# A mixture-of-experts stretch: splits one load later in the program, rows brought back later, evacuations one piece behind

## The chip, the cores and the metric

The kernel runs on one core of a Trainium2 chip. A core has a matrix engine (TensorE, PE in the profile), a vector engine (VectorE, DVE), a scalar engine (ScalarE, ACT), GpSimd (POOL) and a sync engine (SyncE, SP) that starts transfers here. The engines run side by side, each in the order of its own program, and wait for each other by semaphores. The metric is the device time of one execution in microseconds (us).

## The reference

Two decoder layers over 256 positions of width 1024, in float32. Layer 0 mixes with windowed attention beside a short convolution and then applies a dense SwiGLU. Layer 1 mixes with a gated linear recurrence and then applies a mixture of eight experts, two for each position. All that the change touches lies in the last part:

```python
top_logits, top_idx = lax.top_k(xf @ w_router, 2)
gates = softmax(top_logits)
# for each expert e, over the positions that chose it:
hb = silu(xb @ w_gate[e]) * (xb @ w_up[e])     # (rows,1024)@(1024,3584), twice
yb = hb @ w_down[e]                            # (rows,3584)@(3584,1024)
out = x + sum over the two chosen experts of gate * yb
```

The weights of the eight experts are 8 x 3 x 1024 x 3584 numbers of 4 bytes, 352 MB, and each is read once.

## The kernel before, in words

Each float32 operand is written as a high part H, rounded to the matrix engine's fp32r type by an ACT copy, and a low part L, the rest, by a DVE subtraction. A product is then a few fp32r matmuls (H with H, H with L, L with H).

The experts are sorted by how many positions chose them. Three get room for 128 rows and are called heavy (turns 0, 3 and 6 of the program), five get 64 rows and are called light (turns 1, 2, 4, 5 and 7). In a light expert H and L of the rows stand beside each other in the 128 columns, so that a weight chunk needs four matmuls for each piece, in a heavy one six. The hidden width 3584 is cut in seven parts f of 512. The program's list `order` holds the 56 (expert, f) items: three heavy items first, then cycles of light, heavy, light.

The weights of an item are six loads of 1 MB (two each for gate, up and down), and each load feeds two pieces. The list `pieces` holds, for each item, four gate pieces, four up pieces, and then the four down pieces of the item before, so a cycle of three items is 36 pieces or 18 loads. The main loop (L1203 and after) issues for each piece n, in this order: its matmuls (`products`), the evacuations of a finished gate or up bank (`follow`), whatever was put off to this piece (`later`, filled by `at`), and the splits of the next loads, as many as `AHEAD` allows (`prepare`). This part of the kernel is under a manual schedule: each engine gets its instructions in just that order. So the place of a split relative to the small operations is a matter of the code, and an ACT or DVE operation that waits for TensorE holds up every split behind it.

- `prepare` and `hl_of` (L256, L257): the split of one load, an ACT copy of 128x2048 into H and a DVE subtraction into L. H and L come from four pairs of buffers (`N_HL`), and a pair is free when the matmuls of its load are done.
- The loads land in seven 1 MB buffers in turn (five of the ring `w` and two of `b`). SP issues a transfer (L205, L961) when the DVE subtraction of the load that had the buffer before is done.
- `follow`: for a heavy item Silu out of the gate bank (L1147) and a DVE product with the up bank (L1156), then `turn` five pieces after the last up piece, which transposes the hidden part into the shape of a left operand. For a light item copies out of both banks (L1149, L1160), then `turn_light` five pieces after (matmuls L1103, Silu L1105, product L1106) and `split_light` nine pieces after (L256 and L257 on `b`). The down pieces, 13 to 16 pieces after, read the result.
- When the last down pieces of an expert are done, `out_parts` scales and splits its output (ACT L1121, DVE L1122), and `combine` brings its rows back to their positions (matmuls L1129 and L1130 into a `pz` bank) and adds them into x (DVE L1132). Four such quarters follow an expert, one and two pieces after each half of `out_parts`.
- `gather` (matmuls L1025 and L1035, copies L1027 and L1038), `factors` and `back` prepare the next expert's rows, selection factors and transposed selection.
- There are two `pz` banks for all of these, four `pa` banks for the outputs of the experts under way, and two `pw` banks for gate and up.

Of the kernel before, what the change touches and what calls it, by code (L numbers as in the profile page):

```python
# [14 lines left out]
AF = mybir.ActivationFunctionType  # L15
# [5 lines left out]
S = 256  # L21
# [10 lines left out]
N_HL = 4  # L32
# [17 lines left out]
FAR = 1024  # L50


AHEAD = N_HL
FIRST = 1
SECOND = 2
TURN = 5

TURNS8 = N_RING + 2
TURNS4 = TURNS8 + 2
# [54 lines left out]
def body(ctx, tc, x_d, w_d, prm_d, bv_d, rt_d, out_d):  # L114
# [33 lines left out]
    def pz():  # L148
        return psp.tile([P, 512], F32, tag="z", name=nm("pz"))
# [761 lines left out]
    def experts(rest):  # L911
# [30 lines left out]

        parts = {}
        loads = len(pieces) // 2
        later = {}
        regs = {}
        sel, xg, fac, pts, psum, hid, ys, yp = {}, {}, {}, {}, {}, {}, {}, {}
# [67 lines left out]
        def gather(u, b):  # L1015

            ps = units[u]
            o = (pa if ps[0] == 0 and not rest else pz)()
            if ps[0] in heavy:

                a, b = b // 2, b % 2
                for j in range(4):
                    d = (4 * b + j) * P
                    for t in R2:
                        T.matmul(o[:, j * P:(j + 1) * P], (xh3, xl3)[a][:, t, d:d + P], sel_of(ps[0], t),  # L1025
                                 start=t == 0, stop=t == 1)
                A.activation(xg[ps[0]][a][:, b * 512:(b + 1) * 512], o, AF.Copy)  # L1027
                return

            o = o[:, 0:256 * len(ps)].rearrange("p (e j a s) -> p e j a s", e=len(ps), j=2, a=2)  # L1030
            for j in R2:
                d = (2 * b + j) * P
                for a in R2:
                    for t in R2:
                        T.matmul(o[:, :, j, a, :], (xh3, xl3)[a][:, t, d:d + P], sel[u][:, t, :, 0:64],  # L1035
                                 start=t == 0, stop=t == 1)
            for e, p in enumerate(ps):
                A.activation(xg[p][:, b * 256:(b + 1) * 256], o[:, e, :, :, :].rearrange("p j a s -> p (j a s)"), AF.Copy)  # L1038

        def factors(p, cols):  # L1040

            o = pz()
            sc = scl if rest or p == 0 else sclp
            for t in R2:
                T.matmul(o[:, cols], sel_of(p, t).bitcast(F32), sc[:, t, p, cols], start=t == 0, stop=t == 1)
            if p not in fac:
                fac[p] = sm.tile([P, 2], F32, tag="gs", name=nm("gs"), bufs=6)
            V.tensor_copy(fac[p][:, cols], o[:, cols])

        def back(p):  # L1050

            o = pz()
            for t in R2:
                T.transpose(o[:, t * P:(t + 1) * P], sel_of(p, t).bitcast(F32), ident)
            pt = b1(F32R)
            A.activation(pt, o[:, 0:S], AF.Copy)
            pts[p] = pt
# [9 lines left out]
        def products(n):  # L1067
            m, p, f, i = pieces[n]
            h, l = parts.pop(n)
            if m in "gu":  # L1070
                if i == 0:
                    psum[m] = pw()
                for j in range(2):
                    c = slice(j * 512, (j + 1) * 512)
                    k = 2 * i + j
                    r = slice(k * P, (k + 1) * P)
                    a = (xg[p][0][:, r], xg[p][1][:, r]) if p in heavy else xg[p][:, r]
                    mm(psum[m], a, h[:, c], l[:, c], k == 0, k == KC - 1)
            else:
                if f == 0 and i == 0:  # L1080
                    ys[p] = pa(), pa()
                for j in R2:
                    k = 2 * (i % 2) + j
                    r = slice(k * P, (k + 1) * P)
                    o = slice(j * 512, (j + 1) * 512)
                    a = (hid[p, f][0][:, r], hid[p, f][1][:, r]) if p in heavy else hid[p, f][:, r]
                    mm(ys[p][i // 2], a, h[:, o], l[:, o], f == 0 and k == 0, f == NF - 1 and k == 3)

        def turn(p, f, sg):
            o = pz()  # L1090
            for k in range(4):
                T.transpose(o[:, k * P:(k + 1) * P], sg[:, k * P:(k + 1) * P], ident)
            hh, hlo = b2(F32R), b2(F32R)
            hl_of(o, hh, hlo)
            hid[p, f] = hh, hlo

        def turn_light(p, f, g, u):

            o = pz()
            for j, src in enumerate((g, u)):  # L1100
                for k in range(4):
                    c = j * S + k * 64
                    T.matmul(o[:, c:c + 64], src[:, k * P:(k + 1) * P], ii, start=True, stop=True)  # L1103
            s = b2()
            A.activation(s[:, 0:S], o[:, 0:S], AF.Silu)  # L1105
            V.tensor_mul(s[:, S:], o[:, S:], s[:, 0:S])  # L1106
            hid[p, f] = s

        def split_light(p, f):
            h = b2(F32R)  # L1110
# [4 lines left out]
        def out_parts(p, c):  # L1115

            gs = fac[p][:, 0:1]
            if c == 0:
                yp[p] = b4(F32R), b4(F32R)
            yh, yl = (y[:, c * 512:(c + 1) * 512] for y in yp[p])  # L1120
            A.activation(yh, ys[p][c], AF.Copy, scale=gs)  # L1121
            V.scalar_tensor_tensor(yl, ys[p][c], gs, yh.bitcast(F32), OP.mult, OP.subtract)  # L1122

        def combine(p, i):
            yh, yl = yp[p]
            o = pz()
            for j in range(2):
                d = slice((2 * i + j) * P, (2 * i + j + 1) * P)
                T.matmul(o[:, j * S:(j + 1) * S], yh[:, d], pts[p], start=True, stop=False)  # L1129
                T.matmul(o[:, j * S:(j + 1) * S], yl[:, d], pts[p], start=False, stop=True)  # L1130
            v = x_sb[:, 2 * i:2 * i + 2, :]
            V.tensor_add(v, k3(o, 2), v)  # L1132
            if p == order[-1][0]:
                q = (nc.sync, nc.scalar)[i % 2]
                q.dma_start(out_d[:, i * 512:(i + 1) * 512].rearrange("p (k s) -> p k s", k=2), v)

        def at(n, fn, *a):
            later.setdefault(min(n, len(pieces) - 1), []).append((fn, a))

        def follow(n):  # L1140

            m, p, f, i = pieces[n]
            if m == "g" and i == 3:
                sg = b2()
                if p in heavy:

                    A.activation(sg, psum["g"], AF.Silu, scale=fac[p][:, 1:2])  # L1147
                else:
                    A.activation(sg, psum["g"], AF.Copy, scale=fac[p][:, 1:2])  # L1149
                psum["sg"] = sg  # L1150
            elif m == "u" and i == 3:
                sg = psum["sg"]

                last = (p, f) == order[-1]
                if p in heavy:
                    V.tensor_mul(sg, psum["u"], sg)  # L1156
                    at(n + (1 if last else TURN), turn, p, f, sg)
                else:
                    u = b2()
                    A.activation(u, psum["u"], AF.Copy)  # L1160
                    at(n + (1 if last else TURN), turn_light, p, f, sg, u)
                    at(n + (3 if last else TURN + 4), split_light, p, f)
            elif m == "d" and i % 2 and f == NF - 1:
                out_parts(p, i // 2)
                for j in R2:
                    at(n + 1 + j, combine, p, i - 1 + j)

        if not rest:
            at(1, places)
# [15 lines left out]
        with tc.manual_schedule():  # L1185
            for n in range(FIRST):
                prepare(n)
            if not rest:
                router(3)
                low = by_token(3)  # L1190
                choices()

                A.activation(rw[:, 4, 0, 0:1], ones[:, 0:1], AF.Silu)
            choose(0)
            if not rest:
                squares(3)
            for n in range(FIRST, SECOND):
                prepare(n)
            for b in (0, 2):
                gather(0, b)  # L1200
            if not rest:
                low()
            ready = SECOND  # L1203
            for n in range(len(pieces)):
                products(n)
                if n == 1:
                    for b in (1, 3):
                        gather(0, b)
                if n == 0 and not rest:
                    norm()  # L1210
                if n == 3:
                    factors(0, slice(1, 2))
                follow(n)
                for fn, a in later.pop(n, ()):
                    fn(*a)
                while ready < min((n + 1) // 2 + AHEAD, SECOND + n + 1, loads):
                    prepare(ready)
                    ready += 1
# [97 lines left out]
```

## Time and profile before

| what | value |
|---|---|
| median of 3 runs | 1376.69 us (1376.37 to 1381.61) |
| the profiled execution's own time | 1379.48 us |
| its span in the profile | 1377.7 us |
| TensorE busy, share of the span | 95% |
| VectorE busy | 83% |
| ScalarE busy | 71% |
| read from memory | 424.77 MB, 309 GB/s over the span |

The profiled execution took 2.8 us more than the median of the runs, and 1.8 us of its time lie outside the span. A busy TensorE is not a full one, since the ends of matmuls are modelled: one of 512 columns is shown with some 390 ns, though the next one starts 0.23 us after it.

How the views below are read. The windows view gives for each stretch its length, then for PE, PE's weight loads, DVE, ACT and POOL the busy time with the number of instructions, then the granted TensorE clock as a share, the busy share of the DMA engines, and the GB/s that they moved. The transfers by line give the number of issues, the size of one and the median us from issue to landing. The chain of waits gives the start, the length and the line of each step of the chain that ended last. The timeline gives start, length, engine, line and tiles of instructions in order, and in brackets the idle time before it with what ended it. The waits give who waited for whom, the us in total, how often, and the longest.

### The profile page before, as it was taken

The page shows a single profiled execution, that of the slowest core. Times are in us where ns is not written, and L with a number is a line of the kernel's source. Part 1 is how long each engine was busy: PE and PEld are TensorE (multiplying, and loading weights), DVE is VectorE, ACT ScalarE, POOL GpSimd, SP SyncE. Part 2 cuts the span into 40 slices and gives each one's busy share as a digit, 9 for nine tenths or more (in the row PEclk, how much of TensorE's full clock was granted, in tenths as well). Part 3 has the DMA queues.
Part 4 walks back from the last instruction along what each step waited for, and adds up shares of the span by engine and source line. Part 5 has one row for each costly group of instructions (what it writes and reads, how often), then busy time and mean ns, then how long its engine had stood idle before and what let it go on. Part 6 is the DMA issues. An engine that isn't in the chain of part 4 may idle for free.

```text
span 1377.7 us, 19891 instructions
## 1 busy us (share of the span) xinstructions
PE 1303.7 (95%) x7727; PEld 1140.7 (83%) x7727; DVE 1137.9 (83%) x1051; ACT 976.4 (71%) x939; POOL 4.2 (0%) x29
## 2 busy tenths in 40 slices
PE   8999999999998999999899999999989999999997
PEld 7799999999998778778678777777768878787775
DVE  6677655555786789999989998999988999989996
ACT  6445444444587678898778888788867887878893
POOL 1000000000000000000000000000000000000000
PEclk9999999999999999999999999999999999999999
DMA  7444555555434579999989999999998999989992
GB/s 293 145 147 168 186 182 183 183 181 183 173 122 183 215 279 375 419 421 421 420 299 382 422 420 393 351 414 420 419 397 306 382 421 421 405 327 422 421 418 80
DMA packets 61446, 427.19 MB, mean 310 GB/s; under 512 B 7200, under 2 KB 7200, under 8 KB 11296
## 3 DMA queue, kind: packets, MB, share of 16 engines
q1 hardware_dynamic: 60624, 425.22, 78.1%
q8 instruction: 62, 1.02, 0.3%
q10 hardware_dynamic: 720, 0.62, 0.1%
q14 instruction: 40, 0.33, 0.1%
HBM read 424.77 MB, written 1.05 MB: 309 GB/s over the span
## 4 chain that ended last, share of the span: by engine, by line
PE 67%; DVE 15%; issue 9%; ACT 8%; DMA 0%; DVEq 0%; SPq 0%; ACTq 0%
DVE L L257 11%; PE pw L236 9%; PE pw L237 9%; PE pw L238 9%; ACT H L256 4%; PE pz L1103 4%; PE pw L1064 3%; PE pa L237 3%; PE pw L1065 3%; PE pa L238 3%; PE pa L236 3%; PE pa L319 3%; PE pa L317 3%; PE pa L318 3%; PE pa L1064 3%
## 5 line engine op out<-in xcount | busy, mean ns | idle before, releaser
L257 DVE TENSOR_TENSOR L<-w,H 128x2048 fp32r<-128x2048 f32 (+1 forms) x243 | 537.8, 2241 | 53.9 <-ACT H L256 53.4
L256 ACT ACTIVATE H<-w 128x2048 fp32r<-128x2048 f32 (+1 forms) x243 | 452.3, 1877 | 52.8 <-PE pw L238 25.5
L231 ACT ACTIVATE H<-w 128x1024 fp32r<-128x1024 f32 (+1 forms) x138 | 140.2, 1039 | 153.7 <-issue 139.9
L257 DVE TENSOR_TENSOR L<-b,H 128x2048 fp32r<-128x2048 f32 (+1 forms) x102 | 222.1, 2200 | 12.0 <-ACT H L256 11.8
L1064 PE MATMUL pw<-H,b 128*128 128x512 f32 x560 | 222.2, 397 | 0.0
L1065 PE MATMUL pw<-L,b 128*128 128x512 f32 x560 | 218.5, 390 | 0.0
L232 DVE TENSOR_TENSOR L<-w,H 128x1024 fp32r<-128x1024 f32 (+1 forms) x138 | 164.1, 1205 | 56.1 <-ACT H L231 56.1
L256 ACT ACTIVATE H<-b 128x2048 fp32r<-128x2048 f32 (+1 forms) x102 | 187.0, 1844 | 16.6 <-PE pw L238 8.8
L236 PE MATMUL pw<-b,H 128*128 128x256 f32 x672 | 191.6, 286 | 2.1 <-DVE b L622 1.1
L237 PE MATMUL pw<-b,H 128*128 128x256 f32 x672 | 191.3, 285 | 0.0
L238 PE MATMUL pw<-b,L 128*128 128x256 f32 x672 | 191.2, 285 | 0.0
L1064 PE MATMUL pa<-H,b 128*128 128x512 f32 x280 | 113.7, 406 | 26.3 <-DVE b L257 26.3
L236 PE MATMUL pw<-H,b 128*128 128x512 f32 x336 | 133.8, 398 | 0.3 <-ACT b L1147 0.2
L237 PE MATMUL pw<-L,b 128*128 128x512 f32 x336 | 131.2, 391 | 1.2 <-DVE L L257 1.2
L236 PEld LDWEIGHTS pw<-b,H 128*128 128x128 f32 x672 | 129.6, 193 | 3.2 <-issue 2.8
L238 PE MATMUL pw<-H,b 128*128 128x512 f32 x336 | 131.2, 390 | 0.2 <-ACT b L1027 0.2
L237 PEld LDWEIGHTS pw<-b,H 128*128 128x128 f32 x672 | 129.6, 193 | 0.2
L238 PEld LDWEIGHTS pw<-b,L 128*128 128x128 f32 x672 | 129.8, 193 | 0.0
L1064 PEld LDWEIGHTS pw<-H,b 128*128 128x128 f32 x560 | 105.3, 188 | 20.4
L1065 PEld LDWEIGHTS pw<-L,b 128*128 128x128 f32 x560 | 105.3, 188 | 20.2
L1065 PE MATMUL pa<-L,b 128*128 128x512 f32 x280 | 110.4, 394 | 0.0
L319 PE MATMUL pa<-b,L 128*128 128x256 f32 x352 | 99.6, 286 | 2.7 <-DVE L L232 2.7
(250 smaller groups left out, 1947.7 us busy)
## 6 DMA issues: line engine op xcount, KB each, us to landing
w<-in_w_dram SPq DMA_DIRECT2D x297, 1024.0 KB, 7.7
b<-in_w_dram SPq DMA_DIRECT2D x94, 1024.0 KB, 8.2
w<-in_w_dram SPq DMA_DIRECT2D x12, 512.0 KB, 8.3
b<-in_w_dram SPq DMA_DIRECT2D x8, 512.0 KB, 8.6
w<-in_w_dram SPq DMA_DIRECT2D x4, 768.0 KB, 8.1
x_sb<-in_x_dram SPq DMA_DIRECT2D x4, 256.0 KB, 7.7
out_dram<-x_sb SPq DMA_DIRECT2D x2, 256.0 KB, 2.9
out_dram<-x_sb ACTq DMA_DIRECT2D x2, 256.0 KB, 2.9
```

What stands on the lines that cost most here:

```text
L231: A.activation(h, w[:, c], AF.Copy)
L232: V.tensor_sub(l, w[:, c], h.bitcast(F32))
L236: T.matmul(o, a[0], b[0], start=first, stop=False)
L237: T.matmul(o, a[0], b[1], start=False, stop=False)
L238: T.matmul(o, a[1], b[0], start=False, stop=last)
L256: A.activation(oh, src, AF.Copy)
L257: V.tensor_sub(ol, src, oh.bitcast(F32))
L317: T.matmul(o, h[:, c], m[0][:, ks[i], :], start=f and d % 2 == 0, stop=False, skip_group_check=True)
L319: T.matmul(o, l[:, c], m[0][:, ks[i], :], start=False, stop=z and d % 2 == 1, skip_group_check=True)
L1064: T.matmul(o, a, h, start=first, stop=False)
L1065: T.matmul(o, a, l, start=False, stop=last)
L1103: T.matmul(o[:, c:c + 64], src[:, k * P:(k + 1) * P], ii, start=True, stop=True)
```

## The change

`AHEAD` goes from four to three: after piece n the loads up to number (n+1)//2+2 have been split in the programs, not up to (n+1)//2+3. Each operation of `follow` and `later` therefore stands one split earlier among the splits on ACT and DVE. The buffers stay as they are, and so does the order of the transfers. `split_light` moves from nine to eight pieces after the last up piece. The quarters of `combine` go from one and two pieces after a half of `out_parts` to five and seven pieces (first half) and seven and nine pieces (second half), but for those of the last experts. Silu and product of `turn_light` and the copies of `gather` are put into a list `pend`, which is emptied after the matmuls of the next piece, or one at a time when a new `pz` bank is wanted while two are pending. No instruction is added or taken away on any engine.

```diff
-AHEAD = N_HL
+AHEAD = N_HL - 1
+BACK = 5
...
+        pend = []
+        def flush():
+            while pend:
+                pend.pop(0)()
+        def zz():
+            if len(pend) > 1:
+                pend.pop(0)()
+            return pz()
...
         def gather(u, b):
-            o = (pa if ps[0] == 0 and not rest else pz)()
+            now = ps[0] == 0 and not rest
+            o = pa() if now else zz()
...
-                A.activation(xg[ps[0]][a][:, b * 512:(b + 1) * 512], o, AF.Copy)
+                pend.append(lambda: A.activation(xg[ps[0]][a][:, b * 512:(b + 1) * 512], o, AF.Copy))
+                if now:
+                    flush()
...
         def turn_light(p, f, g, u):
-            o = pz()
+            o = zz()
...
             s = b2()
-            A.activation(s[:, 0:S], o[:, 0:S], AF.Silu)
-            V.tensor_mul(s[:, S:], o[:, S:], s[:, 0:S])
             hid[p, f] = s
+            def out():
+                A.activation(s[:, 0:S], o[:, 0:S], AF.Silu)
+                V.tensor_mul(s[:, S:], o[:, S:], s[:, 0:S])
+            pend.append(out)
...
-                    at(n + (3 if last else TURN + 4), split_light, p, f)
+                    at(n + (3 if last else TURN + 3), split_light, p, f)
             elif m == "d" and i % 2 and f == NF - 1:
                 out_parts(p, i // 2)
+                end = n + BACK + 7 >= len(pieces)
                 for j in R2:
-                    at(n + 1 + j, combine, p, i - 1 + j)
+                    at(n + (1 + j if end else BACK + 2 * j + i - 1), combine, p, i - 1 + j)
...
             for n in range(len(pieces)):
                 products(n)
+                flush()
```

In the listings of the engines' orders, L256 and L257 of before are L258 and L259 of the change; L1121, L1122, L1132, L1147 and L1156 are L1147, L1148, L1158, L1173 and L1182. A number behind a name tells tiles apart.

The first place is on ACT, in the cycle in which the first light expert ends: the Silu of a heavy item, the light item's `split_light` (the 128x4x64 copy), splits, and the first half of `out_parts`. Before:

```order
L256 ACTIVATE H_6618<-w_6616 128x2048
L1147 ACTIVATE b_840_6634<-pw_6591,gs_5084 128x512
L256 ACTIVATE H_6638<-w_6636 128x2048
L256 ACTIVATE b_845_6649<-b_836_6607 128x4x64
L256 ACTIVATE H_6663<-w_6661 128x2048
L256 ACTIVATE H_6686<-w_6684 128x2048
L1121 ACTIVATE b_855_6698<-pa_5685,gs_5394 128x512
```

With the change, at the same place:

```order
L1173 ACTIVATE b_837_6628<-pw_6585,gs_5078 128x512
L258 ACTIVATE b_838_6630<-b_833_6601 128x4x64
L258 ACTIVATE H_6635<-w_6633 128x2048
L258 ACTIVATE H_6654<-w_6652 128x2048
L258 ACTIVATE H_6680<-w_6678 128x2048
L1147 ACTIVATE b_852_6692<-pa_5679,gs_5388 128x512
```

The down pieces of the light item multiply with the loads H_6618 and H_6638 before, H_6635 and H_6654 with the change. `split_light` stood behind the splits of both and now stands ahead of both.

The second place is on DVE, from the first half of that `out_parts` on (the rows into `b` out of `pa`), with the splits and the additions into x. Before:

```order
L257 TENSOR_TENSOR L_6687<-w_6684,H_6686 128x2048
L1122 SCALAR_TENSOR_TENSOR b_856_6699<-pa_5685,gs_5394,b_855_6698 128x512
L257 TENSOR_TENSOR L_6705<-b_857_6702,H_6704 128x2048
L1132 TENSOR_TENSOR x_sb<-pz_6712,x_sb 128x512
L1122 SCALAR_TENSOR_TENSOR b_856_6699<-pa_5686,gs_5394,b_855_6698 128x512
L1132 TENSOR_TENSOR x_sb<-pz_6724,x_sb 128x512
L257 TENSOR_TENSOR L_6733<-b_862_6730,H_6732 128x2048
L257 TENSOR_TENSOR b_868_6747<-pz_6741,b_867_6746 128x512
L1132 TENSOR_TENSOR x_sb<-pz_6750,x_sb 128x512
L1132 TENSOR_TENSOR x_sb<-pz_6760,x_sb 128x512
```

With the change:

```order
L259 TENSOR_TENSOR L_6681<-w_6678,H_6680 128x2048
L1148 SCALAR_TENSOR_TENSOR b_853_6693<-pa_5679,gs_5388,b_852_6692 128x512
L259 TENSOR_TENSOR L_6699<-w_6696,H_6698 128x2048
L1148 SCALAR_TENSOR_TENSOR b_853_6693<-pa_5680,gs_5388,b_852_6692 128x512
L259 TENSOR_TENSOR L_6715<-b_857_6712,H_6714 128x2048
L259 TENSOR_TENSOR b_863_6729<-pz_6723,b_862_6728 128x512
L259 TENSOR_TENSOR L_6739<-b_864_6736,H_6738 128x2048
L1158 TENSOR_TENSOR x_sb<-pz_6746,x_sb 128x512
L259 TENSOR_TENSOR L_6761<-w_6758,H_6760 128x2048
L1158 TENSOR_TENSOR x_sb<-pz_6778,x_sb 128x512
```

The four additions stood with one split of a load among them, and the first ahead of the second half of `out_parts`. Now the first comes two splits of loads after that half, and a split stands between each two.

## Rows read from the trace of the kernel before

**Rows 1.** Windows: length, busy by engine, clock, DMA share, GB/s

```profile
7.50:20.00 12.50, 11.26 (x49) 9.74 (x50) 10.76 (x19) 11.69 (x19) 0.00 (x0) 0.73 1.03 421
1240.00:1242.50 2.50, 2.50 (x13) 2.07 (x12) 2.50 (x3) 2.02 (x3) 0.00 (x0) 1.00 1.03 436
578.00:623.00 45.00, 43.05 (x206) 35.40 (x206) 42.62 (x25) 38.32 (x29) 0.00 (x0) 1.00 1.01 421
545.00:1345.00 800.00, 755.57 (x3684) 623.32 (x3684) 742.28 (x449) 659.61 (x508) 0.00 (x0) 1.00 0.98 396
680.00:725.00 45.00, 38.91 (x208) 31.73 (x207) 39.85 (x32) 33.61 (x30) 0.00 (x0) 1.00 0.85 326
850.00:895.00 45.00, 41.25 (x205) 33.78 (x204) 40.86 (x28) 36.52 (x29) 0.00 (x0) 1.00 0.94 359
1010.00:1065.00 55.00, 49.06 (x252) 40.27 (x250) 47.77 (x36) 40.76 (x35) 0.00 (x0) 0.97 0.86 333
1195.00:1225.00 30.00, 26.59 (x126) 21.82 (x125) 25.90 (x20) 21.23 (x17) 0.00 (x0) 0.94 0.85 336
```

**Rows 2.** Transfers by line, from 200 to 260 us, then 900 to 1000

```profile
w<-in_w_dram SPq DMA_DIRECT2D x10, 1024.0 KB, 4.8
...
w<-in_w_dram SPq DMA_DIRECT2D x29, 1024.0 KB, 8.9
```

**Rows 3.** Chain of waits, the same step of first, second and last cycle

```profile
533.63 1.73 PE pz L1103 x16
...
578.45 1.73 PE pz L1103 x16
...
1342.59 1.73 PE pz L1103 x16
```

**Rows 4.** Chain of waits, within the cycle that starts at 578.45

```profile
580.18 0.28 PE pw L236
...
580.70 0.23 PE pw L238
...
586.59 0.23 PE pw L237
...
617.99 0.50 PE pa L1064
```

**Rows 5.** Timeline of DVE in the same cycle

```profile
601.64 11.09 DVE L257 TENSOR_TENSOR L<-w,H 128x2048 fp32r<-128x2048 f32 x5
...
617.51 0.42 DVE L257 TENSOR_TENSOR b<-b,b 128x256 fp32r<-128x256 f32 x1
```

**Rows 6.** Waits, 533 to 1343 us

```profile
PE pa L1064 <- DVE b L257: 26.3, 17, 1.6
...
PE pz L1130 <- DVE b L1122: 9.0, 4, 2.7
...
PE pa L237 <- DVE L L257: 4.3, 13, 0.3
...
PE pz L1129 <- DVE b L257: 2.9, 2, 1.6
```

**Rows 7.** Timeline of PE where two experts end

```profile
685.21 0.38 PE L1130 MATMUL pz<-b,b 128*128 128x256 f32 x1 [2.73 <-DVE b L1122]
...
686.59 0.28 PE L1129 MATMUL pz<-b,b 128*128 128x256 f32 x1
...
687.06 0.40 PE L1064 MATMUL pw<-H,b 128*128 128x512 f32 x1
...
695.59 1.00 PE L1025 MATMUL pz<-b,b 128*128 128x128 f32 x8
...
696.43 0.45 PE L1064 MATMUL pw<-H,b 128*128 128x512 f32 x1
```

**Rows 8.** Timeline of ACT in the cycle that starts at 578.45

```profile
595.75 1.92 ACT L256 ACTIVATE H<-b 128x2048 fp32r<-128x2048 f32 x1
...
601.84 0.58 ACT L1160 ACTIVATE b<-pw 128x512 f32<-128x512 f32 x1
```

More of the change, by code (lines that the diff above doesn't have):

```diff
@@ L1036, in gather @@
                                  start=t == 0, stop=t == 1)
-            for e, p in enumerate(ps):
-                A.activation(xg[p][:, b * 256:(b + 1) * 256], o[:, e, :, :, :].rearrange("p j a s -> p (j a s)"), AF.Copy)
+            def out():
+                for e, p in enumerate(ps):
+                    A.activation(xg[p][:, b * 256:(b + 1) * 256], o[:, e, :, :, :].rearrange("p j a s -> p (j a s)"),
+                                 AF.Copy)
+            pend.append(out)
         def factors(p, cols):
-            o = pz()
+            o = zz()
             sc = scl if rest or p == 0 else sclp
@@ L1050, in back @@
         def back(p):
-            o = pz()
+            o = zz()
             for t in R2:
@@ L1089, in turn @@
         def turn(p, f, sg):
-            o = pz()
+            o = zz()
             for k in range(4):
@@ L1097, in turn_light @@
         def turn_light(p, f, g, u):
-            o = pz()
+            o = zz()
             for j, src in enumerate((g, u)):
@@ L1104, in turn_light, with out @@
             s = b2()
-            A.activation(s[:, 0:S], o[:, 0:S], AF.Silu)
-            V.tensor_mul(s[:, S:], o[:, S:], s[:, 0:S])
             hid[p, f] = s
+            def out():
+                A.activation(s[:, 0:S], o[:, 0:S], AF.Silu)
+                V.tensor_mul(s[:, S:], o[:, S:], s[:, 0:S])
+            pend.append(out)
         def split_light(p, f):
@@ L1125, in combine @@
             yh, yl = yp[p]
-            o = pz()
+            o = zz()
             for j in range(2):
@@ L1205, in experts @@
                 products(n)
+                flush()
                 if n == 1:
@@ L1208, in experts @@
                         gather(0, b)
+                    flush()
                 if n == 0 and not rest:
```

## Prediction, written before the changed kernel ran

> **What bounds the kernel now.** I read the windows first, then the transfers, the chain of waits, the waits, and last the timelines at the places that the waits named. The windows show two kinds of stretch between 545 and 1345 us. In a plain cycle of heavy, light, light the transfers move 421 GB/s, and so they did in the first 20 us, when all buffers were free and a row of loads stood waiting [rows 1]. A load takes 4.8 us from issue to landing in the dense part and 8.9 us here [rows 2], so some 4 us of every load are queueing behind other loads. I read 421 GB/s as the rate that the transfers can't pass. A cycle is 18 loads of 1.0486 MB, 18.87 MB, and at 421 GB/s that is 44.8 us. The chain of waits has the same step, the transposes of a light item, at 533.63 and at 578.45, which is 44.82 us [rows 3].
>
> The four stretches in which experts end move 326, 359, 333 and 336 GB/s [rows 1]. Against 421 they lose 10.2, 6.6, 11.5 and 6.1 us (the missing share times the length). The whole from 545 to 1345 has 396 GB/s, which is (1 - 396/421) x 800 = 47.5 us lost. The chain agrees: 1342.59 - 533.63 = 808.96 us for 17 cycles is 47.0 more than 17 x 44.82 [rows 3]. These 47 us are what there is to win between the two, as long as 421 stands.
>
> Why is it not won now, when data are there? The other engines have hardly any slack. TensorE starts a matmul of 512 columns every 0.2265 us (5.89 us for 26 of them) and needs 1.73 us for the transposes of a light item [rows 3, 4]. A cycle has 72 heavy and 96 light matmuls, 38.05 us, two light transposes with 0.05 us more behind them, 3.56, and the heavy item's four transposes, estimated at 0.4: 42.0 us. DVE does five splits in 11.09 us, 2.2 each [rows 5]; 18 of them are 39.6 us, and the small products and subtractions (0.42 us for the light one [rows 5], some 0.6 for the heavy) bring it to about 42. So TensorE could do a cycle in 42.0 us, 2.8 less than the loads need, and could catch up after a bad stretch. It doesn't: it waits for `split_light` (17 waits in the matmuls, 26.3 us) and for L at the heavy down pieces (4.3 us), 30.6 us or 1.8 us a cycle [rows 6]. In the cycle from 578 us this is seen at 617.99, where TensorE goes on just after DVE did `split_light` at 617.51, behind splits that had kept DVE busy without a gap since 601.64 [rows 4, 5]. TensorE thus takes as long as the loads do even where the loads are ahead.
>
> **The change part by part.** No instruction comes or goes, so only waits and orders count.
>
> `AHEAD` three and `split_light` a piece earlier: by the order rows of the change, `split_light` stood behind the splits of both loads that its own down pieces read, and now stands ahead of both. DVE reaches it two splits sooner, 2 x 2.2 = 4.4 us, and the wait that it caused was at most 1.6 us [rows 6]. It goes; what is late next is the split of the down pieces' own load, which DVE, busy all along, delivers about when TensorE asks for it. So of the 2.8 us a cycle that TensorE doesn't work now, between 0 and 2.8 come free. I take 1.2, nearer the lower end, since DVE needs about 42 us itself. In plain cycles this gives nothing, since the loads' 44.8 us cover it. Its worth is that TensorE can catch up after an expert's end.
>
> A rule of the Trainium skill speaks against that: its page "Perfetto Trace Analysis", section "Optimization Strategy", says that a gap repeating on the engine that should be full can mean too few buffers. The wait of 1.6 us comes back in each cycle, and by that rule it would stay, since four pairs stay four; the 1.2 would be 0. The trace bears it out in part only: what TensorE waits for is the small split, not a free pair. The case is the second rival.
>
> Rows brought back later: the waits of `combine` for the scaled halves are 9.0 us, and for its first operand's splits 2.9 us [rows 6]; one of them is the 2.73 us at 685.21 [rows 7]. With 5 to 9 pieces between they go. What may come instead is a wait for one of the two `pz` banks: each addition into x now stands behind a split of a load that TensorE needs four matmuls later, so a quarter can hold TensorE back by up to 4 x 0.2265 us and the addition, some 1.5 us. Six experts end inside the window, 24 quarters; the bound is a loss of 24 x 1.5 = 36 if every one meets it, and a gain of 11.9. Most fall where TensorE is behind DVE, as in heavy pieces, so I take waits of 1 us in all, a gain of 11.
>
> The work itself stays. A quarter takes 686.59 to 687.06, 0.47 us, and a gather group 0.84 us [rows 7]. 24 quarters are 11.3, 16 groups 13.4, and selection and factors an estimated 4, together 29 us of TensorE beside the cycles. How much of it hides? After a plain stretch the seven buffers can take the loads on while TensorE is late: two are being split, two are on their way (4.8 us at 2.5 us a load), so three, 7.5 us, are cover. The ends come in four groups, with about 3.5 cycles between them, in each of which 1.2 us are caught up: 4.2 us. The first group hides up to 7.5, the next three 4.2 each, 20 in all; I take 17, as cover is lost where a group is long. The bounds are 0 and 29.
>
> Silu and gather copies one piece behind: they move past one piece's matmuls in the code, but a split is issued only after every second piece, and they come before it as they did. Cost 0; it could be up to 0.4 us an item either way, which the slack of a cycle covers. SP's order of transfers is untouched. The end of the program keeps its order of rows brought back, and the first heavy items have no light one before them: 0 for both, with 3 us on either side.
>
> Sum: 11 + 17 = 28 us less. The profiled execution took 1379.5, so 1351.5; it lies 2.8 above the median of the runs, so 1349.
>
> **The rivals.**
>
> Everything hides. TensorE follows the loads at 421 GB/s throughout: 47.5 less, and some 4 at the end since TensorE is closer behind the last load: 1379.5 - 51 - 2.8 = 1326. For it speaks that TensorE's own work, 17 x 42.0 + 29 = 743, is below the 762 of the loads; against it that both, and DVE, are so near each other that every wait shows.
>
> Only the waits of the rows brought back go, and the plain cycle's wait is merely renamed. Then nothing is caught up, and 11 us remain: 1366.
>
> Nothing moves. The additions into x hold the `pz` banks and give back the 11: 1377. For it speaks that there are still two banks for more uses at once.
>
> The loads go faster than I read. One short window has 436 GB/s [rows 1], and the seven buffers, not the transfers, might set the 421. Then the cycle is 43.3, and TensorE's 743 us decide, 66 less than 809: 1311. The first 20 us and the queueing speak against it. The page "DMA: Bandwidth & Descriptors" of the Trainium skill, section "Specifications", gives 435 GB/s as the ceiling, which would be a cycle of 43.4; no stretch of a cycle's length here reaches it.
>
> Slower: three loads ahead is too short. At the copy out of a light item's gate or up bank ACT waits for TensorE, and behind it only four pieces stand split, not six. These take TensorE 16 x 0.2265 = 3.6 us. The copy, the next split's two halves, 0.58 + 1.92 [rows 8] + 2.2, take 4.7. If ACT is really held there, TensorE then lacks 1.1 us, four times a cycle: 42.0 + 4.4 = 46.4 us, 1.6 over now, 28 over 17.8 cycles, less the 11: 1394. It decides from 0.7 us at each copy on (42.0 + 2.8). Against it: DVE still has a split in hand when ACT is held, and where loads set the pace ACT comes to the copy after TensorE.
>
> **How the numbers follow.** Chances: the forecast 0.50 (its own range 1336 to 1364), everything hides 0.11, faster loads 0.02, only the rows brought back 0.12, nothing moves 0.14, slower 0.11. The range 1329 to 1380 leaves out the slower case and most of the faster loads and of everything hidden. 0.5% is 6.9 us, about what a measurement can tell from no change. Faster by more: 0.50 + 0.11 + 0.02 and three quarters of 0.12 (its `pz` waits may take some back), 0.72. Within: 0.17. Slower: 0.11.
>
> **What would show it.** Right: matmuls of L1086 (L1064 before) into `pa` no longer wait for DVE's `b`; the matmuls of `combine` wait under 3 us in all; plain cycles still take 44.8 us and 421 GB/s; the four stretches of ends rise above 370 GB/s; and some waits of ACT for a landing load appear, as a sign that the loads set the pace. Wrong: plain cycles longer than 45 us, with TensorE waiting for L at gate and up pieces (the slower case), or the ends as deep as before, with TensorE waiting for additions into x.

## The result and the profile after

The changed kernel takes 1412.97 us (median of 4 runs, 1411.47 to 1416.72) against 1378.04 of the kernel before on the same chip: 1.0254 times as long, 95% interval 1.0223 to 1.0285. It is slower by 2.5%, where the forecast was 2% faster, and lies outside the range. The span of its profiled execution is 1414.9 us.

The windows of the changed kernel, with the columns of [rows 1] (the last two are the DMA share and GB/s): the whole stretch of the experts, a plain cycle, and the two stretches in which two experts end together.

```profile
545.00:1385.00 840.00, 784.57 (x3710) 621.14 (x3709) 750.29 (x452) 654.12 (x510) 0.00 (x0) 1.00 0.96 380
578.00:623.00 45.00, 43.33 (x201) 34.09 (x202) 40.23 (x23) 35.09 (x27) 0.00 (x0) 1.00 0.99 399
690.00:740.00 50.00, 43.75 (x231) 35.75 (x229) 42.94 (x33) 35.09 (x31) 0.00 (x0) 0.97 0.82 307
1045.00:1095.00 50.00, 43.91 (x232) 36.51 (x232) 42.56 (x33) 33.81 (x31) 0.00 (x0) 0.97 0.84 310
```

A plain cycle now moves 399 GB/s, where it moved 421, and the double ends 307 and 310, where [rows 1] have 326 and 333. The chain of waits, at the same step as [rows 3] (the light transposes have line L1125 now), for the first cycle, the second, and the seventeenth:

```profile
536.20 1.73 PE pz L1125 x16
...
583.68 1.73 PE pz L1125 x16
...
1332.01 1.73 PE pz L1125 x16
```

A plain cycle takes 583.68 - 536.20 = 47.48 us instead of 44.82. Sixteen cycles take 795.81 us, 36.1 more than 16 x 47.48; before it was 47.0 more than 16 x 44.82. So the ends of experts did become 11 us cheaper against their own cycles, and each plain cycle 2.66 us dearer: 17 x 2.66 - 11 = 34, close to the 34.9 between the medians. Experiments 2 and 3 show that most of the 11 comes with the longer cycles and not from the rows brought back later. The loads don't set this pace. From 900 to 1000 us they take less from issue to landing than the 8.9 us of [rows 2], which fits a shorter queue:

```profile
w<-in_w_dram SPq DMA_DIRECT2D x25, 1024.0 KB, 7.5
```

The waits of the changed kernel in the stretch of the cycles (who waited for whom, us in total, times, longest):

```profile
DVE L L259 <- ACT H L258: 80.7, 78, 2.7
ACT b L1130 <- PE pz L1125: 74.6, 34, 3.3
...
ACT b L1173 <- PE pw L240: 34.6, 17, 2.5
ACT b L258 <- PE pz L1114: 22.6, 14, 2.4
PE pw L1087 <- DVE L L259: 21.5, 34, 1.0
ACT b L1175 <- PE pw L1087: 20.4, 34, 1.4
PE pa L1087 <- DVE L L259: 19.4, 15, 1.3
...
ACT H L258 <- PE pa L1086: 0.3, 2, 0.2
```

Of before, the waits in the same stretch that these answer to:

```profile
ACT b L1105 <- PE pz L1103: 36.0, 34, 1.6
ACT H L256 <- PE pw L238: 31.8, 33, 1.5
ACT H L256 <- PE pa L238: 18.4, 30, 0.8
ACT b L1147 <- PE pw L238: 14.7, 17, 1.3
```

ACT's wait for the light transposes (L1130, L1105 before) went from 36.0 to 74.6 us, that for the heavy gate bank (L1173, L1147 before) from 14.7 to 34.6, and its waits at L258 for the heavy transposes are new among the long ones. ACT's waits for a free pair H, 31.8 and 18.4 us before, are gone but for 0.3. TensorE's wait for `split_light` [rows 6] is gone too, and in its place TensorE waits for L at ordinary pieces (L1087 into `pw` and `pa`).

How one of these goes round is seen in the cycle that starts at 583.68. ACT's timeline:

```profile
581.26 1.91 ACT L258 ACTIVATE H<-b 128x2048 fp32r<-128x2048 f32 x1
585.45 0.38 ACT L1130 ACTIVATE b<-pz 128x256 f32<-128x256 f32 x1 [2.28 <-PE pz L1125]
585.73 1.91 ACT L258 ACTIVATE H<-b 128x2048 fp32r<-128x2048 f32 x1
589.62 0.69 ACT L1173 ACTIVATE b<-pw,gs 128x512 f32<-128x512 f32 x1 [1.98 <-PE pw L240]
...
601.24 0.60 ACT L258 ACTIVATE b<-pz 128x512 fp32r<-128x512 f32 x1 [1.61 <-PE pz L1114]
...
617.39 0.39 ACT L1130 ACTIVATE b<-pz 128x256 f32<-128x256 f32 x1 [2.45 <-PE pz L1125]
617.67 1.91 ACT L258 ACTIVATE H<-w 128x2048 fp32r<-128x2048 f32 x1
620.18 0.69 ACT L1175 ACTIVATE b<-pw,gs 128x512 f32<-128x512 f32 x1 [0.60 <-PE pw L1087]
```

DVE in the same cycle, at the last of those places:

```profile
609.07 8.99 DVE L259 TENSOR_TENSOR L<-w,H 128x2048 fp32r<-128x2048 f32 x4
617.98 0.42 DVE L1131 TENSOR_TENSOR b<-pz,b 128x256 f32<-128x256 f32 x1
619.61 2.29 DVE L259 TENSOR_TENSOR L<-w,H 128x2048 fp32r<-128x2048 f32 x1 [1.22 <-ACT H L258]
...
623.01 4.49 DVE L259 TENSOR_TENSOR L<-b,H 128x2048 fp32r<-128x2048 f32 x2 [0.77 <-ACT H L258]
```

TensorE's waits in the same cycle:

```profile
599.80 0.50 PE L1087 MATMUL pw<-L,b 128*128 128x512 f32 x1 [0.69 <-DVE L L259]
...
607.00 0.50 PE L1087 MATMUL pw<-L,b 128*128 128x512 f32 x1 [0.69 <-DVE L L259]
...
625.36 0.50 PE L1087 MATMUL pa<-L,b 128*128 128x512 f32 x1 [1.29 <-DVE L L259]
```

ACT finishes a split, comes to the Silu of a light item and sits idle for 2.28 us at one and 2.45 us at the next, until TensorE has done the transposes. The split behind the Silu could have run all the while. DVE, which had work until 618.4, then lacks H for 1.22 us. TensorE does not feel this yet: its prepared pieces last until that split is done at 621.9. But ACT is held again, for 0.60 us, at the copy out of the light gate bank (620.18). DVE lacks H for another 0.77 us (623.01), and now TensorE lacks L, for 1.29 us at 625.36. The first stop spends what was in hand, and the second finds nothing left. In this cycle DVE is idle 4.1 us for H of a load and 0.7 for H of `split_light`; in a plain cycle of before it was 2.3. The 2.5 us more are nearly the whole of the 2.66.

### The profile page after: what moved, and what is told of

Same layout as the page of the kernel before. It is cut to its first block, busy times and chain, and to the rows that moved or that the text cites. A ratio compares the mean times of both kernels' runs of the same rounds, so it can differ in the third digit from the quotient of the medians.

```text
span 1414.9 us, 19916 instructions
## 1 busy us (share of the span) xinstructions
PE 1330.2 (94%) x7727; PEld 1136.4 (80%) x7727; DVE 1141.1 (81%) x1051; ACT 967.0 (68%) x939; POOL 4.2 (0%) x29
## 4 chain that ended last, share of the span: by engine, by line
PE 61%; DVE 16%; ACT 12%; issue 9%; DMA 0%; DVEq 0%; SPq 0%; ACTq 0%
DVE L L259 14%; PE pw L239 9%; PE pw L238 9%; PE pw L240 9%; ACT H L258 8%; PE pz L1125 4%; PE pa L239 3%; PE pa L240 3%; PE pw L1086 3%; PE pa L238 3%; PE pw L1087 3%; PE pa L321 3%; PE pa L319 3%; PE pa L320 3%; ACT H L233 1%
## 5 line engine op out<-in xcount | busy, mean ns | idle before, releaser
L259 DVE TENSOR_TENSOR L<-w,H 128x2048 fp32r<-128x2048 f32 (+1 forms) x243 | 537.2, 2243 | 70.7 <-ACT H L258 70.3
L258 ACT ACTIVATE H<-w 128x2048 fp32r<-128x2048 f32 (+1 forms) x243 | 445.7, 1873 | 0.3 <-PE pa L1086 0.3
L1087 PE MATMUL pw<-L,b 128*128 128x512 f32 x560 | 226.3, 404 | 22.0 <-DVE L L259 21.6
L259 DVE TENSOR_TENSOR L<-b,H 128x2048 fp32r<-128x2048 f32 (+1 forms) x102 | 222.3, 2203 | 22.5 <-ACT H L258 22.4
L258 ACT ACTIVATE H<-b 128x2048 fp32r<-128x2048 f32 (+1 forms) x102 | 185.2, 1842 | 0.1
L1087 PEld LDWEIGHTS pw<-L,b 128*128 128x128 f32 x560 | 106.1, 189 | 64.7 <-DVE L L259 45.6
L239 PE MATMUL pw<-L,b 128*128 128x512 f32 x336 | 133.8, 398 | 5.7 <-DVE L L259 4.7
L1087 PE MATMUL pa<-L,b 128*128 128x512 f32 x280 | 114.3, 408 | 20.8 <-DVE L L259 19.4
L1086 PE MATMUL pa<-H,b 128*128 128x512 f32 x280 | 110.0, 393 | 0.0
L320 PE MATMUL pa<-b,H 128*128 128x256 f32 x352 | 101.2, 288 | 1.2 <-DVE b L259 1.2
```

Source lines behind the costliest of these rows:

```text
L239: T.matmul(o, a[0], b[1], start=False, stop=False)
L258: A.activation(oh, src, AF.Copy)
L259: V.tensor_sub(ol, src, oh.bitcast(F32))
L320: T.matmul(o, h[:, c], m[1][:, ks[i], :], start=False, stop=False, skip_group_check=True)
L1086: T.matmul(o, a, h, start=first, stop=False)
L1087: T.matmul(o, a, l, start=False, stop=last)
```

## The experiments

Each ran beside the kernel before on the same chip: 1 to 4 on one chip, 5 to 8 on a second, 9 to 11 on a third. The medians of the kernel before on them, and beside the change, lie between 1376.8 and 1378.0 us. The ends are what the first sixteen cycles take beyond sixteen times the first, plain one.

| kernel | median us | ratio to before, 95% interval | plain cycle us | ends us |
|---|---|---|---|---|
| the change | 1412.97 | 1.0254 [1.0223, 1.0285] | 47.48 | 36 |
| 1: change, four ahead | 1351.7 | 0.9806 [0.9781, 0.9830] | 43.09 | 49 |
| 2: before, three ahead | 1419.67 | 1.0301 [1.0276, 1.0325] | 47.55 | 39 |
| 3: before, rows back later | 1374.21 | 0.9977 [0.9967, 0.9986] | 44.84 | 43 |
| 4: change, evacuations and turns later | 1370.23 | 0.9944 [0.9926, 0.9962] | 44.87 | 41 |
| 5: before, split_light earlier | 1356.25 | 0.9848 [0.9823, 0.9872] | 43.08 | 54 |
| 6: as 1, split_light as before | 1374.39 | 0.9974 [0.9963, 0.9985] | 44.86 | 42 |
| 7: change, only bank readers later | 1353.01 | 0.9818 [0.9801, 0.9834] | 43.13 | 52 |
| 8: as 1, rows back from six | 1344.43 | 0.9770 [0.9747, 0.9794] | 43.08 | 41 |
| 9: as 1, rows back from eight | 1339.99 | 0.9728 [0.9712, 0.9744] | 43.11 | 38 |
| 10: as 8, bank copies later | 1341.21 | 0.9737 [0.9721, 0.9753] | 43.24 | 38 |
| 11: change, two ahead | 1641.84 | 1.1920 [1.1889, 1.1951] | - | - |

**1. The change with four ahead.** Theory A was read off the profile after: an operation of ACT that waits for TensorE stands one split too early. Theory B was its rival: the rows brought back later hold the two `pz` banks.

```diff
-AHEAD = N_HL - 1
+AHEAD = N_HL
```

> The change with AHEAD back at four and everything else of it kept. Theory A (small ACT operations that wait for TensorE stand one split too early): the plain cycle goes from 47.5 back to 44.8 us, the ends of experts stay 11 us cheaper than before, so about 1413 - 45 = 1366 us. Theory B (the late rows and the evacuations a piece behind hold the two pz banks): the cycle stays at 47.5 and the time at about 1413.

It took 1351.7 us, faster than either theory said, and 61 us less than the change. B falls: `AHEAD` is what cost. Whether it costs by the place of ACT's operations, as A has it, or by the depth itself, this run can't tell (4 and 7 can). The chain of waits has the first cycle, the second and the seventeenth at

```profile
533.62 1.73 PE pz L1125 x16
...
576.71 1.73 PE pz L1125 x16
...
1272.32 1.73 PE pz L1125 x16
```

so a plain cycle takes 43.09 us, not the 44.8 that I expected it to go back to. Nor do the ends stay 11 us cheaper: they take 49 us. In its waits, ACT waits 12.8 us for the light transposes in place of 74.6, and something appears that the kernel before doesn't have, ACT waiting for a load to land:

```profile
ACT b L1130 <- PE pz L1125: 12.8, 18, 1.2
...
ACT H L258 <- DMA w<-in_w_dram: 6.3, 14, 0.6
```

Its windows, between two groups of ends, in the middle of a double end, and over the whole of that end:

```profile
910.00:990.00 80.00, 79.21 (x377) 65.35 (x376) 78.46 (x45) 71.17 (x52) 0.00 (x0) 1.00 1.01 421
...
1010.00:1020.00 10.00, 6.01 (x24) 5.01 (x23) 8.26 (x7) 5.06 (x5) 0.00 (x0) 0.73 1.01 421
...
990.00:1050.00 60.00, 53.66 (x270) 45.34 (x270) 50.95 (x39) 44.58 (x39) 0.00 (x0) 0.94 0.91 367
```

Over 80 us with no end of two experts it moves 421 GB/s, the same as before, though its plain cycles would use 18.87 MB / 43.09 us = 438. It lives on loads that landed during the ends, and catches up, as the prediction had it; when they are used up it waits for landings.

**2. Three ahead alone**, on the kernel before.

```diff
-AHEAD = N_HL
+AHEAD = N_HL - 1
```

> The kernel before with AHEAD three as its only edit. Theory A: the plain cycle is 47 us or more, the ends cost 47 us as before, so 1377 + 17 x 2.7 = about 1423 us, 10 slower than the whole change. Theory B: no slower than before, 1377 or less.

1419.67 us, 43 more than before and 7 more than the whole change. The first two cycles:

```profile
535.00 1.73 PE pz L1103 x16
...
582.55 1.73 PE pz L1103 x16
```

47.55 us a cycle with neither the late rows nor anything in `pend`: `AHEAD` alone makes the cycle longer. The ends take 39 us here, 8 less than before, with the rows brought back as early as before. So of the 11 us by which the change has cheaper ends, some 8 come with the longer cycle. I read it so: where a cycle is longer than TensorE's own work, more of the work of the ends hides in it.

**3. The rows brought back later alone.** The edit is that of `BACK` and `end` in the change, on the kernel before.

> The kernel before with only the rows brought back five pieces on. Theory A: plain cycles of 44.8 us as before and 11 us less at the ends of experts, about 1366 us. Theory B: the plain cycle has no rows brought back in it, but the ends get longer, 1377 or more.

1374.21 us: 2.7 us gained, not 11. The waits for the scaled halves are gone, but in their place TensorE waits for a free `pz` bank, at the rows brought back (for an addition into x), at a gather group (for the split of the heavy transposes) and at the selection (for the factors):

```profile
PE pz L1130 <- DVE x_sb L1133: 4.8, 4, 1.7
...
PE pz L1026 <- DVE b L258: 4.5, 2, 2.2
...
PE pz L1055 <- DVE gs L1049: 2.0, 3, 0.9
```

Together that is 11.3 us, about as much as the 11.9 that went. The last two kinds were 0 and 0.2 us in the kernel before.

**4. Three ahead, evacuations of both banks, turns and `split_light` two pieces later.**

```diff
+            LATE = 2
...
-                    A.activation(sg, psum["g"], AF.Silu, scale=fac[p][:, 1:2])
+                at(n + LATE, g_out, psum["g"], sg)
...
-                    at(n + (1 if last else TURN), turn_light, p, f, sg, u)
+                    at(n + (1 if last else TURN + LATE), turn_light, p, f, sg, u)
```

> The change, still three ahead, but the evacuations of the gate and up banks, turn, turn_light and split_light all stand two pieces, that is one split, later. Theory A, if the place among the splits is what counts: ACT is held with six pieces split behind it again, the cycle goes back to about 44.8 us, about 1366 us. If three loads ahead is too few in itself, whatever stands between them: it stays at about 1413.

1370.23 us, 43 less than the change, with the cycle at

```profile
533.84 1.73 PE pz L1125 x16
...
578.71 1.73 PE pz L1125 x16
```

44.87 us, but 18 us above four ahead. ACT's wait for the light transposes has not gone:

```profile
ACT b L1130 <- PE pz L1125: 85.5, 34, 3.9
```

That was my mistake in the experiment, and a useful one. Moving `turn_light` moves its transposes along with the Silu that waits for them, so as many pieces stand split between the two as in the change. What counts is not the place of the operation alone but how many pieces are split beyond the one that it waits for. The copies out of the gate and up banks, whose matmuls stayed, got their distance back: ACT's waits for these banks, 34.6 and 20.4 us in the rows of the change, are gone from the trace. I put down 43 of the 61 us to them.

**5. `split_light` one piece earlier alone**, on the kernel before.

```diff
-                    at(n + (3 if last else TURN + 4), split_light, p, f)
+                    at(n + (3 if last else TURN + 3), split_light, p, f)
```

> The kernel before with split_light eight instead of nine pieces after the last up piece as its only edit, so still four ahead and rows brought back at once. If this step alone takes away TensorE's wait at the light down pieces, the plain cycle falls from 44.8 to about 43.1 us as with four ahead and the rest of the change (1351.7), and the time to about 1355 us. If the evacuations one piece behind did it, it stays at 1377.

1356.25 us, with a cycle of 43.08:

```profile
533.38 1.73 PE pz L1103 x16
...
576.46 1.73 PE pz L1103 x16
```

This one piece gains 20.6 us, since with four ahead it brings the operation ahead of a split. TensorE's wait for `split_light`, 26.3 us before [rows 6], is gone. So it was not the loads that kept a plain cycle at 44.8 us.

**6. The change with four ahead and `split_light` back at nine pieces.** Edits: those of 1, and the reverse of 5.

> The change with four ahead, and split_light back at nine pieces: what is left is the rows brought back later and the evacuations one piece behind. If split_light is what gained, about 1374 us as with the rows alone and plain cycles of 44.8 us. If the evacuations one piece behind gained, about 1352 us.

1374.39 us, the same as the late rows alone (1374.21): with four ahead the evacuations one piece behind are worth nothing.

**7. Three ahead, matmuls in place, everything that reads their banks two pieces later.** As 4, but the transposes stay at five pieces, and only what reads them moves.

```diff
-            pend.append(out)
+            at(n, out)
...
-                    at(n + (1 if last else TURN), turn_light, p, f, sg, u)
+                    at(n + (1 if last else TURN), turn_light, p, f, sg, u, n + (1 if last else TURN + LATE))
```

> The change, three ahead, with all matmuls and transposes in their places, but every ACT and DVE operation that reads their banks (copies and Silu out of gate and up, the evacuations of turn and turn_light, split_light) two pieces, one split, later. Theory A, that the count of pieces split behind an operation held for TensorE is what costs: like four ahead, 1352 to 1358 us, and ACT's waits for the light transposes fall from 75 us to under 20. If three ahead costs by itself: 1370 as with the transposes moved along, or more.

1353.01 us, 1.3 above four ahead. The first two cycles, and ACT's wait for the light transposes:

```profile
532.11 1.73 PE pz L1125 x16
...
575.24 1.73 PE pz L1125 x16
```

```profile
ACT b L1130 <- PE pz L1125: 11.6, 17, 1.2
```

Three ahead costs next to nothing by itself. Some 60 of the 61 us are the distance between a matmul and the operation held for it, measured in pieces split: 43 for the bank copies, and the remaining 17 for what follows the transposes.

**8 and 9. Four ahead, rows brought back from six, then from eight pieces on.**

```diff
-BACK = 5
+BACK = 6
```

> The change with four ahead, and the rows brought back from six pieces on instead of five, so that a quarter of them falls between two gather groups and not beside one. If the two pz banks hold TensorE at the double ends (waits of 1.2 to 2.5 us seen there), about 1346 us; if those waits follow from DVE being late anyway, 1352 as before.

> Four ahead with the rows brought back from eight pieces on. If falling between the gather groups is what helped at six, the same 1344 us or a little less; if the distance from out_parts helped, lower than 1342. The transfers' pace of 421 GB/s with nothing lost would be about 1326.

1344.43 and 1339.99 us. At five pieces a quarter of the rows stands right beside a gather group and takes the second `pz` bank; at six and eight it stands between two groups. At eight a further 4 us go, and the time lies below the 1342 that I had named as the sign of distance. In experiment 9 the window of the double end moves more than the 367 GB/s of experiment 1:

```profile
990.00:1050.00 60.00, 57.06 (x299) 47.74 (x298) 55.56 (x42) 48.09 (x41) 0.00 (x0) 1.00 1.00 403
```

The clock column shows a second possible cause. In experiment 1 TensorE is busy for 6.01 of the 10 us from 1010 to 1020, where it waits for banks, and its granted clock there has a mean of 0.73: full at first, then at its lower level (0.50, 1.2 GHz) from 1014.6 to 1021.4 us. From 545 to 1300 us the trace has 13.7 us at that level in experiment 1, 3.4 in 8 and none in 9, whose clock over the double end is 1.00. In that stretch matmuls of 512 columns start every 0.43 us, elsewhere every 0.23. So nearly half of such a stretch is lost. I estimate that this can make up to 5 of the 7 us between 1 and 8, and up to 2 of the 4 between 8 and 9. How much of the gain is the clock and how much the waits themselves, no run separates.

Experiment 9 is the fastest kernel of this study: 2.7% faster than before, 5% faster than the change.

**10. As 8, with the bank copies one split later still.** The edit is that of 4 for the two banks only.

> Four ahead and rows from six pieces on, with the copies and the Silu out of the gate and up banks one split later still, so that eight pieces are split behind them. ACT's waits for gate banks go, but ACT then waits for a free pair H, since there are four. If those copies still held DVE up at four ahead: about 1340 us. If the free pair now holds ACT instead: 1344, no change.

1341.21 us against 1344.43, with overlapping intervals: unclear, and at most a small gain, with a plain cycle of 43.24 instead of 43.08. ACT's waits for the heavy gate bank, 12.5 us in experiment 8, are gone, but TensorE now waits 11.2 us at the heavy transposes for DVE's product with the up bank, which this edit moved as well. So the run does not test the copies alone.

**11. Two ahead.**

```diff
-AHEAD = N_HL - 1
+AHEAD = N_HL - 2
```

> The change with AHEAD two. Theory A: with two pieces split behind a copy, 8 matmuls of a light item or 1.8 us, TensorE lacks some 3 us at each of the four light copies and more at the transposes: a plain cycle of 55 us or more, 1530 us or more. If three ahead cost by something that sets in once (a place in the order, a bank), the same 1413.

1641.84 us, more than the 1530 that I gave as a lower bound, with cycles of 58.6 to 62.2 us where no expert ends. Part of it is the clock: its mean is 0.95 from 545 to 1600 us, where the kernel before has 1.00 [rows 1]. A stretch of ACT's timeline shows the waits grown to several us each:

```profile
606.18 0.38 ACT L1130 ACTIVATE b<-pz 128x256 f32<-128x256 f32 x1 [5.31 <-PE pz L1125]
...
624.91 0.60 ACT L258 ACTIVATE b<-pz 128x512 fp32r<-128x512 f32 x1 [4.57 <-PE pz L1114]
...
635.00 0.60 ACT L1186 ACTIVATE b<-pw 128x512 f32<-128x512 f32 x1 [3.01 <-PE pw L1087]
```

## Why the prediction was wrong

The step that failed is "`AHEAD` three and `split_light` a piece earlier", taken together as a gain. The second alone gains 20.6 us (experiment 5); the first alone loses 42.7 (experiment 2), and 61 where the rest of the change is in place (the change against 1). I priced the first at nothing, on the argument that it only brings small operations forward. It does, and that is the loss: they are brought forward past splits, to where TensorE has not yet done what they wait for.

The mechanism stood in the prediction as the slower rival, with a chance of 0.11. I put it aside because DVE would still have a split in hand when ACT is held. The trace shows what becomes of that split: it is spent at the light Silu (DVE worked until 618.4 and then lacked H for 1.22 us), and at the copy that follows TensorE lacks L for 1.29 us. At the second light Silu of a cycle five light pieces stand split, 20 x 0.2265 = 4.5 us of TensorE, and Silu 0.39, split 1.91 + 2.2 and DVE's product 0.42 take 4.9. That is just about even, but ACT is held there too, as at the heavy Silu and the heavy transposes.

The rival's price for the waits, 4.4 us a cycle, came out by luck: 47.48 is 4.4 above the 43.09 of experiment 1. It had put all of it down to the light copies. By experiments 4 and 7 the copies out of the banks, light and heavy, cost 2.6 (47.48 to 44.87) and what follows the transposes 1.7 (44.87 to 43.13). Its sum of 1394 fell short since it started from 42.0 us a cycle, where the shortest cycle measured is 43.08: 1.08 x 17.8 = 19 us, the distance to 1413. The 11 us that it took off at the ends did go, though mostly not by the late rows (experiments 2 and 3).

I had compared one light case, found it tight, and let the average slack of 2.8 us a cycle decide. But engines that wait for each other in a ring have no average slack: in the cycle shown, each of the three was idle in turn.

What held:

- 421 GB/s as the pace of the loads. With the wait for `split_light` gone it is 421 over 80 us, and ACT then waits for landings (experiment 1). Of the windows of 45 us that start every 5 us from 500 to 1295 us, none is above 423 in any run, so the rival of faster loads falls. What did not hold is that a plain cycle must then take 44.8 us: it takes 43.1 in experiments 1, 5, 8 and 9, on loads that landed during the ends.
- TensorE's wait for `split_light` goes, and its worth is catching up after the ends. I took 1.2 us a cycle; it is 44.82 - 43.09 = 1.7. It went without a fifth pair of buffers, so the second rival, in which it stays for want of buffers and nothing is caught up, falls.
- The evacuations one piece behind: 0, as priced (3 against 6).
- The three parts without `AHEAD`: 28 us forecast, 25.3 measured (experiment 1). That this is close is partly luck. The rows brought back were sized wrongly: 11 forecast, 2.7 measured alone, because the banks' waits that I bounded at 36 and took as 1 came out at 11.3 us (experiment 3). The catching up was sized too low: 17 forecast, 20.6 measured alone (experiment 5).

What stays open is why the rows from eight pieces on gain 4 us over six. The distance, the order by the gather groups and the granted clock all change there, and no run separates them. Nor was the Silu's share among the 17 us that follow the transposes taken apart from that of the heavy transposes.

## What to carry to other kernels

On an engine that works in order, ask of every small operation that waits for another engine: how much work for that other engine is already prepared beyond the instruction that it waits for? If that is less than the time to prepare one more piece (here copy 0.6, split 1.9 and 2.2 us against 4 or 5 pieces of 0.9 us), the pipeline stalls, however much slack each engine has on average. Moving an operation past a prefetch in the program changes this distance just as a smaller prefetch depth does; an operation that nobody else waits for soon belongs later, and one that the other engine is about to need belongs earlier.

## What the runs showed of the hardware

The pace of loads is stiff: 421 GB/s when a load took 8.9 us to land, and 421 GB/s over 80 us in experiment 1, where from 900 to 985 us it took 10.8. TensorE's granted clock fell where it had waited: in the bank waits from 1010 us on in experiment 1 it went to 0.50 for 6.8 us, and in experiment 9, with shorter waits at the same double end, it stayed at 1.00. I had not expected how steep the loss is with the prepared distance: 43.1 us a cycle at four ahead, 47.5 at three, and at two a kernel that takes 1642 us, 265 more than before, with the same instructions on every engine.
